# A transformer block in float32 on one core: gate and up projections by one level of Strassen's scheme, on 256 tokens at a time

## The chip, the cores and the metric

The kernel runs on one core of one Trainium2 chip. The metric is the device time of one execution in microseconds (us), lower is better; it is the median of three runs. Shares of a span come from one profiled execution. The core's engines are TensorE (PE, matmuls; its weight loads are shown as PEld), VectorE (DVE), ScalarE (ACT), GpSimd (POOL) and SyncE (SP, which issues most DMAs). They run in parallel, each takes its own instructions in a fixed order, and they wait for each other by semaphores.

## The reference: what is computed

One block of a transformer with 512 tokens and 1024 features: a stick-breaking and a differential attention side by side, gated and projected, then a feed-forward part. The change is in the last two of these lines and in the residual between them:

```python
x = x + einsum('bsd,de->bse', merged, w_out)             # 1024 -> 1024
h2 = _rmsnorm(x, g_ffn)
ff = silu(einsum('bsd,df->bsf', h2, w_ffn_gate)) * einsum('bsd,df->bsf', h2, w_ffn_up)   # 1024 -> 2816
x = x + einsum('bsf,fd->bsd', ff, w_ffn_down)            # 2816 -> 1024
```

Everything is float32.

## The kernel before

Activations are kept with features on the 128 partitions and all 512 tokens along the free axis: x is 8 such blocks, a feed-forward activation 22 (2816 / 128). The 22 are called column tiles below. SBUF is divided by hand: 66 blocks of 128 x 512 in one pool (`B`), 6 buffers of 128 x 1024 for raw weights, and 4 pairs for split weights.

**Float32 as two halves.** PE runs the matmuls on a shorter float format. So each operand is split into h, the rounded value, and l, the rest: `split` (L85) casts on ACT and subtracts on DVE. `mm3` (L202) then makes three matmuls of one product: h by h, h by l, l by h. Activations are split once, weights as they stream in.

**Weights.** `Stream` (L94) holds the list of all weight pieces in order of use, a piece being 128 x 1024, the 8 contraction blocks of one column tile side by side. `next` (L130) splits this piece and the next one and issues the loads of up to 5 further ones on SP's queue.

**The stages that matter here.** In the output projection (L697 to 713), for each of 8 column tiles d, `full_ct(mg)` makes 8 x 3 matmuls of 512 columns into one PSUM bank. DVE adds the old x (loaded again from DRAM) and makes the new residual, which stays in SBUF to the end (`x2`). The norm's gain is multiplied in while the block is split into h2's h and l. ACT squares the block and POOL adds the squares up, for the norm.

In the gate and up stage (L717 to 732), for each of 22 column tiles n, two such products are made, `pg` and `pu`. Behind the first `pg` come the norm's matmul with ones and the factor r2, one per token (L720 to 723). Then DVE multiplies both by r2, ACT applies Silu to one, POOL multiplies the two, and the result is split (L731). In the down stage (L733 to 741), each of 8 output tiles takes 22 x 3 matmuls; DVE adds the residual and the result goes out by DMA.

**Order.** The program gives each instruction its engine. A scheduler orders the instructions of each engine when the program is built, by when it takes their inputs and their buffers to be ready; on the chip this order is fixed. Nothing in these stages is placed by hand.

Of the kernel before, what the change touches and what calls it, by code (L numbers as in the profile page):

```python
# [42 lines left out]
def block_kernel(  # L43
# [40 lines left out]

    def split(h, l, src):  # L85
        a = nc.scalar.copy(out=h, in_=src)  # L86
        b = nc.vector.tensor_tensor(out=l, in0=src, in1=f(h), op=ALU.subtract)  # L87
        return a, b

    def pinned(instrs):  # L90
        for ins in instrs:
            tc.keep_in_program_order(ins)

    class Stream:  # L94
        AHEAD, SPLIT = 5, 2

        def __init__(self, srcs):
            self.srcs, self.raw, self.hl, self.at = srcs, {}, {}, 0
# [8 lines left out]
                    nc.sync.dma_start(out=t[:, :n], in_=src)  # L107

        def split(self, i):
            if i < len(self.srcs) and i not in self.hl:  # L110
                self.load(i)
                t, n = self.raw.pop(i)
                h = wspl.tile([P, 1024], F32R, tag="wh", name=f"wh{i}")
                l = wspl.tile([P, 1024], F32R, tag="wl", name=f"wl{i}")
                split(h[:, :n], l[:, :n], t[:, :n])
                self.hl[i] = (h, l)

        def half(self, kt):
            i, sl = kt // 2, slice((kt % 2) * S, (kt % 2 + 1) * S)
            t, _ = self.raw[i]  # L120
            if kt % 2 == 0:
                h = wspl.tile([P, 1024], F32R, tag="wh", name=f"wh{i}")
                l = wspl.tile([P, 1024], F32R, tag="wl", name=f"wl{i}")
                self.hl[i] = self.part = (h, l)
            h, l = self.part
            pinned(split(h[:, sl], l[:, sl], t[:, sl]))
            if kt % 2:
                self.raw.pop(i)

        def next(self):  # L130
            i = self.at
            self.at += 1
            if i >= KT // 2:
                for j in range(i, i + self.SPLIT):
                    self.split(j)
            for j in range(i, i + self.AHEAD + 1):
                if j not in self.hl:
                    self.load(j)
            return self.hl.pop(i)

    srcs = [w_tc[i, c] for i in range(2) for c in range(4)]
# [22 lines left out]
    for kt in range(KT):  # L164
        t = B(name="xt")
# [521 lines left out]
    for d in range(8):  # L687
        ps = full_ct(o_a)
        nc.vector.tensor_tensor(out=gA[d], in0=gA[d], in1=ps, op=ALU.mult)
        nc.vector.tensor_tensor(out=gA[d], in0=gA[d], in1=mB[d], op=ALU.add)  # L690
        h, l = B(F32R, "mh"), B(F32R, "ml")
        split(h, l, gA[d])
        mg.append((h, l))

    x2, h2 = [], []
    acc = None
    for d in range(8):  # L697
        xr = B(name="xr")
        nc.sync.dma_start(out=xr, in_=xT[:, d])
        ps = full_ct(mg)  # L700
        nc.vector.tensor_tensor(out=xr, in0=ps, in1=xr, op=ALU.add)
        x2.append(xr)
        h, l = B(F32R, "h2h"), B(F32R, "h2l")
        gc = g_ffn[:, d : d + 1]
        nc.scalar.activation(out=h, in_=xr, func=AF.Copy, scale=gc)
        nc.vector.scalar_tensor_tensor(out=l, in0=xr, scalar=gc, in1=f(h), op0=ALU.mult, op1=ALU.subtract)
        h2.append((h, l))
        sq = B(name="x2s")
        nc.scalar.activation(out=sq, in_=xr, func=AF.Square)
        if acc is None:  # L710
            acc = sq
        else:
            nc.gpsimd.tensor_tensor(out=acc, in0=acc, in1=sq, op=ALU.add)

    r2 = B(name="r2")
    ff = []
    for n in range(NF):  # L717
        pg = full_ct(h2)
        if n == 0:
            pn = PS("pn2")  # L720
            nc.tensor.matmul(out=pn, lhsT=ones[:, 0:P], rhs=acc, start=True, stop=True)
            nc.scalar.activation(out=r2, in_=pn, func=AF.Sqrt, scale=1.0 / D, bias=epst)
            nc.vector.reciprocal(out=r2, in_=r2)
        pu = full_ct(h2)
        t1, t2 = B(name="t1"), B(name="t2")
        nc.vector.tensor_tensor(out=t1, in0=pg, in1=r2, op=ALU.mult)
        nc.scalar.activation(out=t1, in_=t1, func=AF.Silu)
        nc.vector.tensor_tensor(out=t2, in0=pu, in1=r2, op=ALU.mult)  # L728
# [75 lines left out]
```

## Time and profile before

| | |
|---|---|
| median of 3 runs (lowest, highest) | 753.12 us (753.03, 753.12) |
| span of the profiled execution, first to last instruction | 751.0 us |
| PE busy, matmuls | 738.1 us (98%), 3406 matmuls |
| PEld busy, weight loads | 611.6 us (81%) |
| DVE busy | 431.8 us (57%) |
| ACT busy | 325.1 us (43%) |
| POOL busy | 103.0 us (14%) |
| DMA | 71.12 MB, 95 GB/s mean |
| granted TensorE clock | 0.998 of 2.4 GHz |

The profiled execution has no time of its own beside its span; the runs' median is 2.1 us above it. An engine's busy time is the union of its instructions' times. Matmuls overlap one another in the records, so PE's pace is read from the starts of its matmuls and not from their durations. In a row of the timeline the first number is the start in us from the start of the span and the second the duration in us; an arrow in square brackets names what ended the engine's idle time before it. L204 is line 204 of the kernel, where a helper's line stands for all its callers; tiles are told by their names, output<-inputs. A row of the windows has the stretch, its length, the busy time (and number of instructions) of PE, PEld, DVE, ACT and POOL in this order, the granted clock as a share of 2.4 GHz, the DMA engines' busy share and GB/s.

### The profile page before, as it was taken

The numbers are of one execution on the slowest core, as the hardware profiler recorded it, in microseconds if no ns is written. First come the engines' busy times: TensorE is split into PE (matmuls) and PEld (weight loads), VectorE is DVE, ScalarE is ACT, GpSimd is POOL, SyncE is SP. The second block draws the span as 40 slices with busy tenths as digits, with TensorE's granted clock in tenths as the row PEclk, the third lists the DMA queues.
The fourth block names the chain that finished last, engine by engine and source line by source line (L and its number), as shares of the span: only waits on it lengthen the run. The fifth ranks groups of instructions, "written<-read, shape, count | busy, mean of one in ns | idle before, by whom it ended". The sixth has DMA issues, their size and how long they took to land.

```text
span 751.0 us, 9018 instructions
## 1 busy us (share of the span) xinstructions
PE 738.1 (98%) x3406; PEld 611.6 (81%) x3406; DVE 431.8 (57%) x648; ACT 325.1 (43%) x514; POOL 103.0 (14%) x139
## 2 busy tenths in 40 slices
PE   8999999999989999999999999999999999999998
PEld 6887887888878878888888888888888888888886
DVE  5856877766687887987446454445545533232220
ACT  6633566877566676544444232323232222222110
POOL 0067000000023223300321011101101111000000
PEclk9999999999999999999999999999999999999999
DMA  8622121211121111244432322332232323333200
GB/s 316 218 98 84 59 83 56 81 61 58 57 84 43 46 39 42 73 152 170 161 120 84 113 84 93 105 103 94 85 112 86 98 83 105 103 118 117 64 14 29
DMA packets 23803, 71.12 MB, mean 95 GB/s; under 512 B 2768, under 2 KB 3408, under 8 KB 23760
## 3 DMA queue, kind: packets, MB, share of 16 engines
q1 hardware_dynamic: 23472, 70.40, 28.0%
q8 instruction: 27, 0.44, 0.2%
q10 hardware_dynamic: 288, 0.15, 0.1%
q14 instruction: 16, 0.13, 0.1%
HBM read 68.44 MB, written 2.10 MB: 94 GB/s over the span
## 4 chain that ended last, share of the span: by engine, by line
PE 89%; DVE 3%; POOL 3%; ACT 2%; issue 2%; DMA 0%; DVEq 0%; POOLq 0%; ACTq 0%
PE pc L204 24%; PE pc L205 24%; PE pc L206 24%; PE pt L221 6%; PE pk L221 3%; PE sc L395 1%; PE sc L394 1%; POOL qn L300 1%; DVE wl L87 1%; PE tb L400 1%; ACT wh L86 1%; PE ta L400 1%; PE av L555 1%; POOL qn L314 1%; PE av L556 1%
## 5 line engine op out<-in xcount | busy, mean ns | idle before, releaser
L86 ACT CAST wh<-raw 128x1024 fp32r<-128x1024 f32 (+2 forms) x136 | 130.9, 963 | 299.1 <-PE pc L205 165.4
L87 DVE TENSOR_TENSOR wl<-raw,wh 128x1024 fp32r<-128x1024 f32 (+2 forms) x136 | 172.7, 1270 | 105.3 <-ACT wh L86 101.2
L204 PE MATMUL pc<-h2h,wh 128*128 128x512 f32 x352 | 137.3, 390 | 0.0
L206 PE MATMUL pc<-h2h,wl 128*128 128x512 f32 x352 | 137.0, 389 | 0.0
L205 PE MATMUL pc<-h2l,wh 128*128 128x512 f32 x352 | 136.9, 389 | 0.0
L204 PE MATMUL pc<-hh,wh 128*128 128x512 f32 x192 | 76.6, 399 | 1.9 <-DVE vs L363 1.5
L205 PEld LDWEIGHTS pc<-h2l,wh 128*128 128x128 f32 x352 | 66.1, 188 | 14.1 <-issue 0.2
L204 PEld LDWEIGHTS pc<-h2h,wh 128*128 128x128 f32 x352 | 66.1, 188 | 14.0 <-issue 0.2
L206 PEld LDWEIGHTS pc<-h2h,wl 128*128 128x128 f32 x352 | 66.1, 188 | 13.5
L206 PE MATMUL pc<-hh,wl 128*128 128x512 f32 x192 | 75.5, 393 | 0.0
L205 PE MATMUL pc<-hl,wh 128*128 128x512 f32 x192 | 75.3, 392 | 0.0
L204 PE MATMUL pc<-fh,wh 128*128 128x512 f32 x176 | 68.5, 389 | 0.0
L205 PE MATMUL pc<-fl,wh 128*128 128x512 f32 x176 | 68.5, 389 | 0.0
L206 PE MATMUL pc<-fh,wl 128*128 128x512 f32 x176 | 68.5, 389 | 0.0
L729 POOL TENSOR_TENSOR t<-t,t 128x512 f32<-128x512 f32 x22 | 30.0, 1363 | 208.5 <-DVE t L728 121.0
L728 DVE TENSOR_TENSOR t<-pc,r 128x512 f32<-128x512 f32 x22 | 15.2, 691 | 67.0 <-PE pc L206 63.2
L204 PEld LDWEIGHTS pc<-hh,wh 128*128 128x128 f32 x192 | 36.4, 190 | 9.2 <-issue 1.7
L206 PEld LDWEIGHTS pc<-hh,wl 128*128 128x128 f32 x192 | 36.2, 189 | 7.8
L205 PEld LDWEIGHTS pc<-hl,wh 128*128 128x128 f32 x192 | 36.4, 190 | 6.7
L530 POOL TENSOR_SCALAR_AFFINE_SELECT om<-om 128x128 f32<-128x128 f32 x32 | 11.4, 356 | 210.4 <-DVE obl L87 138.3
L204 PEld LDWEIGHTS pc<-fh,wh 128*128 128x128 f32 x176 | 33.0, 188 | 6.9
L206 PEld LDWEIGHTS pc<-fh,wl 128*128 128x128 f32 x176 | 33.0, 188 | 6.9
(204 smaller groups left out, 1166.4 us busy)
## 6 DMA issues: line engine op xcount, KB each, us to landing
raw<-w_fg_dram SPq DMA_DIRECT2D x22, 512.0 KB, 3.2
raw<-w_fu_dram SPq DMA_DIRECT2D x22, 512.0 KB, 3.2
raw<-w_gate_dram SPq DMA_DIRECT2D x16, 512.0 KB, 3.2
raw<-w_dn_dram SPq DMA_DIRECT2D x16, 512.0 KB, 3.5
raw<-w_tc_dram SPq DMA_DIRECT2D x12, 512.0 KB, 4.5
raw<-w_ct_dram SPq DMA_DIRECT2D x8, 512.0 KB, 3.3
raw<-w_br_dram SPq DMA_DIRECT2D x16, 256.0 KB, 2.6
raw<-w_out_dram SPq DMA_DIRECT2D x8, 512.0 KB, 3.3
```

What stands on the lines that cost most here:

```text
L86: a = nc.scalar.copy(out=h, in_=src)
L87: b = nc.vector.tensor_tensor(out=l, in0=src, in1=f(h), op=ALU.subtract)
L204: nc.tensor.matmul(out=ps, lhsT=wh, rhs=ah, start=first, stop=False)
L205: nc.tensor.matmul(out=ps, lhsT=wh, rhs=al, start=False, stop=False)
L206: nc.tensor.matmul(out=ps, lhsT=wl, rhs=ah, start=False, stop=last)
L221: nc.tensor.matmul(out=pss[tb], lhsT=hx[:, tb * P : (tb + 1) * P], rhs=wx[:, wsl], start=(kt == 0 and i == 0), stop=(kt == KT - 1 and i == 2),
L300: nc.gpsimd.tensor_tensor(out=q3, in0=q3, in1=gqkt[:, gi : gi + 1, :].broadcast_to([P, 8, 64]), op=ALU.mult,)
L314: nc.gpsimd.tensor_tensor(out=q3[:, :, 0:16], in0=t1, in1=t2, op=ALU.add)
L400: nc.tensor.transpose(out=ps[:, off + (tb - sb) * P : off + (tb - sb + 1) * P], in_=tiles[tb][:, sb * P : (sb + 1) * P], identity=ident,)
L530: nc.gpsimd.affine_select(out=t[:, o + w - P : o + w], in_=t[:, o + w - P : o + w], pattern=[[-1, P]], compare_op=ALU.is_gt, fill=fill, ba ...
L728: nc.vector.tensor_tensor(out=t2, in0=pu, in1=r2, op=ALU.mult)
L729: nc.gpsimd.tensor_tensor(out=t1, in0=t1, in1=t2, op=ALU.mult)
```

## The change: what it does

Two column tiles, gate and up, of the same n form a product of a matrix in 2 x 2 blocks. The activations are cut in two along the contraction (blocks 0 to 3 and 4 to 7) and in two along the tokens (0 to 255, 256 to 511), the weights along the contraction and into up and gate: b11, b21 are up's two halves, b12, b22 gate's. Eight products of 4 blocks and 256 tokens would make it; Winograd's form of Strassen's scheme makes seven, of sums of blocks, and adds up the results.

- **Activations.** Behind the output projection, which takes its column tiles in the order 0, 4, 1, 5, ..., seven operands are built and split: a11, a12, a22 and four sums s1 to s4 (DVE). They hold 28 blocks. The norm's gain is multiplied in on ACT (`y`).
- **Weights.** For each n, `Weights` takes two raw pieces, makes four sums of 512 columns on POOL into two buffers `t13` and `t24` (one of each), and splits up's piece, gate's b22, t13 and t24.
- **Products.** `product` makes 4 x 3 matmuls of 256 columns into half a bank. ACT copies the results of two products to SBUF; DVE, and once POOL, add up the others. Gate's sum comes out negated, which Silu's scale of -1 undoes.
- **Norm.** r2 multiplies gate's sum before Silu; up's r2 is left to the end, where each output of the down stage is multiplied by it (`yo`).
- **ff** is kept whole, and split in a loop behind the 22 tiles. The residual goes to DRAM and is loaded again in the down stage.
- There are 5 raw buffers instead of 6, and 4 pieces are loaded ahead instead of 5.

The core of the diff:

```diff
-N_BLK, N_RAW, N_SPLIT = 66, 6, 4
+N_BLK, N_RAW, N_SPLIT = 66, 5, 4
...
-        AHEAD, SPLIT = 5, 2
+        AHEAD, SPLIT = 4, 2
...
-    x2, h2 = [], []
...
+    half = S // 2
+    lo_t, hi_t = slice(0, half), slice(half, S)
...
+    x2d = nc.dram_tensor("x2_scratch", (KT, P, S), F32, kind="Internal").ap()
...
-    for d in range(8):
+    for d in (0, 4, 1, 5, 2, 6, 3, 7):
         xr = B(name="xr")
         nc.sync.dma_start(out=xr, in_=xT[:, d])
         ps = full_ct(mg)
         nc.vector.tensor_tensor(out=xr, in0=ps, in1=xr, op=ALU.add)
-        x2.append(xr)
-        h, l = B(F32R, "h2h"), B(F32R, "h2l")
-        gc = g_ffn[:, d : d + 1]
-        nc.scalar.activation(out=h, in_=xr, func=AF.Copy, scale=gc)
-        nc.vector.scalar_tensor_tensor(out=l, in0=xr, scalar=gc, in1=f(h), op0=ALU.mult, op1=ALU.subtract)
-        h2.append((h, l))
+        nc.sync.dma_start(out=x2d[d], in_=xr)
+        y = ys[d] = B(name="y")
+        nc.scalar.activation(out=y, in_=xr, func=AF.Copy, scale=g_ffn[:, d : d + 1])
...
+        if d < 4:
+            a11.put(d, y[:, lo_t])
+            continue
+        k = d - 4
+        u, v = ys.pop(k), ys.pop(d)
+        a12.put(k, v[:, lo_t])
+        a22.put(k, v[:, hi_t])
+        sa, sb = B(name="sa"), B(name="sb")
+        nc.vector.tensor_tensor(out=sa[:, lo_t], in0=v[:, hi_t], in1=u[:, hi_t], op=ALU.subtract)
+        nc.vector.tensor_tensor(out=sa[:, hi_t], in0=u[:, lo_t], in1=u[:, hi_t], op=ALU.subtract)
...
+        s1.put(k, sa[:, lo_t])
+        s3.put(k, sa[:, hi_t])
+        s2.put(k, sb[:, lo_t])
+        s4.put(k, sb[:, hi_t])
+
+    class Weights:
+        def __init__(self, n):
+            u, g = ws.take(), ws.take()
+            b11, b21, b12, b22 = u[:, 0:S], u[:, S:1024], g[:, 0:S], g[:, S:1024]
+            t13 = tsum.tile([P, 1024], F32, tag="t13", name=f"t13_{n}")
+            t24 = tsum.tile([P, 1024], F32, tag="t24", name=f"t24_{n}")
+            add = lambda o, a, b: nc.gpsimd.tensor_tensor(out=o, in0=a, in1=b, op=ALU.add)
+            add(t13[:, 0:S], b11, b12)
+            add(t13[:, S:1024], b22, b12)
+            add(t24[:, 0:S], t13[:, 0:S], b22)
+            add(t24[:, S:1024], t24[:, 0:S], b21)
+            uh, ul = self.pair(n, "u")
+            split(uh, ul, u)
+            gh, gl = B(F32R, "gh"), B(F32R, "gl")
+            split(gh, gl, b22)
+            ah, al = self.pair(n, "a")
+            split(ah, al, t13)
+            bh, bl = self.pair(n, "b")
+            split(bh, bl, t24)
...
+    def product(ps, w, a):
+        for kt in range(KT // 2):
+            sl = slice(kt * P, (kt + 1) * P)
+            mm3(ps[:, 0:half], (w[0][:, sl], w[1][:, sl]), a.at(kt), kt == 0, kt == KT // 2 - 1)
...
+    nxt = Weights(0)
     for n in range(NF):
-        pg = full_ct(h2)
+        w = nxt
+        m1 = PS("pc")
+        product(m1, w.b11, a11)
         if n == 0:
             pn = PS("pn2")
...
-        pu = full_ct(h2)
...
+        if n + 1 < NF:
+            nxt = Weights(n + 1)
+        pe, uu, t1, t2 = B(name="pe"), B(name="uu"), B(name="t1"), B(name="t2")
+        nc.scalar.copy(out=pe[:, lo_t], in_=m1[:, 0:half])
+        m5 = PS("m5")
+        product(m5, w.t1, s1)
+        nc.scalar.copy(out=pe[:, hi_t], in_=m5[:, 0:half])
+        m6 = PS("pc")
+        product(m6, w.t2, s2)
+        nc.vector.tensor_tensor(out=uu[:, lo_t], in0=m6[:, 0:half], in1=pe[:, lo_t], op=ALU.add)
+        nc.vector.tensor_tensor(out=t1[:, lo_t], in0=uu[:, lo_t], in1=pe[:, hi_t], op=ALU.add)
+        m7 = PS("m7")
+        product(m7, w.t3, s3)
+        nc.vector.tensor_tensor(out=uu[:, hi_t], in0=m7[:, 0:half], in1=uu[:, lo_t], op=ALU.add)
+        nc.gpsimd.tensor_tensor(out=t1[:, hi_t], in0=uu[:, hi_t], in1=pe[:, hi_t], op=ALU.add)
+        m3 = PS("pc")
+        product(m3, w.b22, s4)
+        nc.vector.tensor_tensor(out=t1[:, lo_t], in0=m3[:, 0:half], in1=t1[:, lo_t], op=ALU.add)
+        nc.vector.tensor_tensor(out=t1, in0=t1, in1=r2, op=ALU.mult)
+        nc.scalar.activation(out=t1, in_=t1, func=AF.Silu, scale=-1.0)
+        m2 = PS("m2")
+        product(m2, w.b21, a12)
+        nc.vector.tensor_tensor(out=t2[:, lo_t], in0=m2[:, 0:half], in1=pe[:, lo_t], op=ALU.add)
+        m4 = PS("pc")
+        product(m4, w.t4, a22)
+        nc.vector.tensor_tensor(out=t2[:, hi_t], in0=m4[:, 0:half], in1=uu[:, hi_t], op=ALU.add)
         nc.gpsimd.tensor_tensor(out=t1, in0=t1, in1=t2, op=ALU.mult)
+        ff.append(t1)
+
+    ws.split(n_down)
+    fs = []
+    for t in ff:
         h, l = B(F32R, "fh"), B(F32R, "fl")
-        split(h, l, t1)
-        ff.append((h, l))
+        split(h, l, t)
+        fs.append((h, l))
     for d in range(8):
+        xr = B(name="xo")
+        nc.sync.dma_start(out=xr, in_=x2d[d])
...
-            nc.vector.tensor_tensor(out=x2[d][:, sl], in0=ps[:, sl], in1=x2[d][:, sl], op=ALU.add)
+            yo = B(name="yo")
+            nc.vector.tensor_tensor(out=yo[:, sl], in0=ps[:, sl], in1=r2[:, sl], op=ALU.mult)
+            nc.vector.tensor_tensor(out=xr[:, sl], in0=yo[:, sl], in1=xr[:, sl], op=ALU.add)
```

## Rows read from the trace of the kernel before

**Rows 1.** Windows by stage: length, then busy time of each engine

```profile
343.70:387.30 43.60, 43.60 (x194) 35.89 (x193) 22.82 (x29) 18.00 (x24) 9.96 (x6) 1.00 0.46 157
387.30:627.50 240.20, 240.20 (x1059) 198.55 (x1058) 120.09 (x111) 74.92 (x92) 30.47 (x22) 1.00 0.29 95
```

**Rows 2.** Timeline of PE in the gate and up stage

```profile
500.40 0.39 PE L204 MATMUL pc<-h2h,wh 128*128 128x512 f32 x1
...
500.63 0.39 PE L205 MATMUL pc<-h2l,wh 128*128 128x512 f32 x1
```

**Rows 3.** Timeline of PE and PEld, 256-column matmuls in the attention part

```profile
229.66 0.28 PE L394 MATMUL sc<-skh,sq 128*128 128x256 f32 x1
229.78 0.28 PE L395 MATMUL sc<-skl,sq 128*128 128x256 f32 x1
...
229.66 0.19 PEld L395 LDWEIGHTS sc<-skl,sq 128*128 128x128 f32 x1
229.78 0.19 PEld L204 LDWEIGHTS pc<-hh,wh 128*128 128x128 f32 x1
```

**Rows 4.** By shape: count, then min/median/max ns, or busy us and mean ns

```profile
L729 POOL TENSOR_TENSOR t<-t,t x22: 1285/1289/2370, 402.2 to 628.6; 128x512 f32<-128x512 f32 x22
...
L314 POOL TENSOR_TENSOR qn<-t,t 128x128 f32<-128x128 f32 x1 | 0.5, 458 | 0.1
...
L87 DVE TENSOR_TENSOR wl<-raw,wh x43: 950/1226/2331, 400.4 to 629.1; 128x1024 fp32r<-128x1024 f32 x42, 128x768 fp32r<-128x768 f32 x1
...
L87 DVE TENSOR_TENSOR fl<-t,fh x21: 676/678/693, 404.1 to 626.2; 128x512 fp32r<-128x512 f32 x21
...
L87 DVE TENSOR_TENSOR tc<-tc,tc 128x256 fp32r<-128x256 f32 x12 | 5.0, 416 | 1.0 <-ACT tc L86 1.0
...
L86 ACT CAST wh<-raw x44: 840/1053/1056, 387.3 to 622.1; 128x1024 fp32r<-128x1024 f32 x43, 128x768 fp32r<-128x768 f32 x1
...
L86 ACT CAST tc<-tc 128x256 fp32r<-128x256 f32 x12 | 4.5, 376 | 4.5 <-PE tc L400 4.5
```

**Rows 5.** Timeline of DVE, then POOL, from 410 us

```profile
410.16 0.69 DVE L728 TENSOR_TENSOR t<-pc,r 128x512 f32<-128x512 f32 x1 [3.31 <-PE pc L206]
411.06 2.30 DVE L87 TENSOR_TENSOR wl<-raw,wh 128x1024 fp32r<-128x1024 f32 x1 [0.21 <-ACT wh L86]
...
411.00 1.29 POOL L729 TENSOR_TENSOR t<-t,t 128x512 f32<-128x512 f32 x1 [7.54 <-DVE t L728]
```

**Rows 6.** Timeline of POOL, then DVE, from 606 us

```profile
606.86 2.37 POOL L729 TENSOR_TENSOR t<-t,t 128x512 f32<-128x512 f32 x1 [9.59 <-ACT wh L86]
...
606.86 1.23 DVE L87 TENSOR_TENSOR wl<-raw,wh 128x1024 fp32r<-128x1024 f32 x1 [0.17 <-ACT wh L86]
```

**Rows 7.** Timeline of DVE, then POOL, from 58.5 us

```profile
58.87 0.68 DVE L296 TENSOR_TENSOR qn<-pk,st 128x512 f32<-128x512 f32 x1
...
58.66 1.28 POOL L300 TENSOR_TENSOR qn<-qn,gqkt 128x512 f32<-128x512 f32 x1
```

**Rows 8.** Timeline of DVE, then ACT, behind the output projection

```profile
387.49 0.69 DVE L701 TENSOR_TENSOR xr<-pc,xr 128x512 f32<-128x512 f32 x1 [2.65 <-PE pc L206]
...
395.83 3.35 DVE L723 RECIPROCAL r<-r 128x512 f32<-128x512 f32 x1 [0.78 <-ACT r L722]
...
388.26 0.72 ACT L705 ACTIVATE h2h<-xr,colt 128x512 fp32r<-128x512 f32 x1
388.89 0.62 ACT L709 ACTIVATE x2s<-xr 128x512 f32<-128x512 f32 x1
```

**Rows 9.** DMA issues: count, KB each, median us to landing

```profile
raw<-w_fg_dram SPq DMA_DIRECT2D x22, 512.0 KB, 3.2
```

**Rows 10.** Windows around two idle times of PE, columns as in rows 1

```profile
217.00:219.20 2.20, 0.00 (x0) 0.00 (x0) 1.88 (x5) 1.08 (x3) 0.82 (x2) 1.00 0.35 136
219.20:222.50 3.30, 3.28 (x12) 2.90 (x13) 2.55 (x4) 2.55 (x5) 0.11 (x1) 0.56 0.28 94
...
269.00:271.80 2.80, 2.01 (x12) 1.62 (x10) 2.42 (x6) 2.75 (x7) 0.42 (x2) 1.00 0.38 94
```

More of the change, by code (lines that the diff above doesn't have):

```diff
@@ L65, in block_kernel @@
     blk = ctx.enter_context(tc.tile_pool(name="blk", bufs=N_BLK))
+    tsum = ctx.enter_context(tc.tile_pool(name="tsum", bufs=1))
     small = ctx.enter_context(tc.tile_pool(name="small", bufs=4))
@@ L109, in split @@
         def split(self, i):
-            if i < len(self.srcs) and i not in self.hl:
+            if i < len(self.srcs) and i not in self.hl and not n_plain <= i < n_down:
                 self.load(i)
@@ L128, in half, with take @@
                 self.raw.pop(i)
+        def take(self):
+            i = self.at
+            self.at += 1
+            for j in range(i, i + self.AHEAD):
+                if j not in self.hl:
+                    self.load(j)
+            return self.raw.pop(i)[0]
         def next(self):
@@ L153, in block_kernel @@
     srcs += [w_br[d, 0] for d in range(8)]
-    srcs += [w_out[d] for d in range(8)]
+    srcs += [w_out[d] for d in (0, 4, 1, 5, 2, 6, 3, 7)]
+    n_plain = len(srcs)
     for n in range(NF):
-        srcs += [w_fg[n], w_fu[n]]
+        srcs += [w_fu[n], w_fg[n]]
+    n_down = len(srcs)
     for d in range(8):
@@ L693, in block_kernel, with __init__, at, put @@
         mg.append((h, l))
-    x2, h2 = [], []
+    half = S // 2
+    lo_t, hi_t = slice(0, half), slice(half, S)
+    class Operand:
+        def __init__(self, name):
+            self.h = [B(F32R, name + "h") for _ in range(2)]
+            self.l = [B(F32R, name + "l") for _ in range(2)]
+        def at(self, kt):
+            sl = slice((kt % 2) * half, (kt % 2 + 1) * half)
+            return self.h[kt // 2][:, sl], self.l[kt // 2][:, sl]
+        def put(self, kt, src):
+            split(*self.at(kt), src)
+    a11, a12, a22 = Operand("a11"), Operand("a12"), Operand("a22")
+    s1, s2, s3, s4 = Operand("s1"), Operand("s2"), Operand("s3"), Operand("s4")
+    x2d = nc.dram_tensor("x2_scratch", (KT, P, S), F32, kind="Internal").ap()
+    ys = {}
     acc = None
-    for d in range(8):
+    for d in (0, 4, 1, 5, 2, 6, 3, 7):
         xr = B(name="xr")
@@ new lines, in block_kernel, with pair @@
+        nc.vector.scalar_tensor_tensor(
+            out=sb[:, lo_t], in0=sa[:, lo_t], scalar=-1.0, in1=u[:, lo_t], op0=ALU.mult, op1=ALU.subtract
+        )
+        nc.vector.scalar_tensor_tensor(
+            out=sb[:, hi_t], in0=v[:, lo_t], scalar=-1.0, in1=sb[:, lo_t], op0=ALU.mult, op1=ALU.subtract
+        )
+        s1.put(k, sa[:, lo_t])
[21 more added lines that the diff above has]
+            split(bh, bl, t24)
+            lo, hi = slice(0, S), slice(S, 1024)
+            self.b11, self.b21 = (uh[:, lo], ul[:, lo]), (uh[:, hi], ul[:, hi])
+            self.b22 = (gh, gl)
+            self.t1, self.t3 = (ah[:, lo], al[:, lo]), (ah[:, hi], al[:, hi])
+            self.t2, self.t4 = (bh[:, lo], bl[:, lo]), (bh[:, hi], bl[:, hi])
+        def pair(self, n, c):
+            return (
+                wspl.tile([P, 1024], F32R, tag="wh", name=f"wh{c}{n}"),
+                wspl.tile([P, 1024], F32R, tag="wl", name=f"wl{c}{n}"),
+            )
@@ L723, in block_kernel @@
             nc.vector.reciprocal(out=r2, in_=r2)
-        pu = full_ct(h2)
[L725 to L728, printed above, removed]
+        if n + 1 < NF:
+            nxt = Weights(n + 1)
+        pe, uu, t1, t2 = B(name="pe"), B(name="uu"), B(name="t1"), B(name="t2")
+        nc.scalar.copy(out=pe[:, lo_t], in_=m1[:, 0:half])
@@ L729, in block_kernel @@
+        m4 = PS("pc")
+        product(m4, w.t4, a22)
+        nc.vector.tensor_tensor(out=t2[:, hi_t], in0=m4[:, 0:half], in1=uu[:, hi_t], op=ALU.add)
         nc.gpsimd.tensor_tensor(out=t1, in0=t1, in1=t2, op=ALU.mult)
+        ff.append(t1)
+    ws.split(n_down)
+    fs = []
+    for t in ff:
         h, l = B(F32R, "fh"), B(F32R, "fl")
-        split(h, l, t1)
-        ff.append((h, l))
+        split(h, l, t)
+        fs.append((h, l))
     for d in range(8):
-        ps = full_ct(ff[0:8], last=False)
@@ L735, in block_kernel @@
-        full_ct(ff[8:16], ps=ps, first=False, last=False)
-        full_ct(ff[16:22], ps=ps, first=False, last=True)
+        xr = B(name="xo")
+        nc.sync.dma_start(out=xr, in_=x2d[d])
+        ps = full_ct(fs[0:8], last=False)
+        full_ct(fs[8:16], ps=ps, first=False, last=False)
+        full_ct(fs[16:22], ps=ps, first=False, last=True)
         parts = 2 if d == 7 else 1
@@ L739, in block_kernel @@
             sl = slice(i * S // parts, (i + 1) * S // parts)
-            nc.vector.tensor_tensor(out=x2[d][:, sl], in0=ps[:, sl], in1=x2[d][:, sl], op=ALU.add)
-            (nc.sync, nc.scalar)[i].dma_start(out=out[d * P : (d + 1) * P, sl], in_=x2[d][:, sl])
+            yo = B(name="yo")
+            nc.vector.tensor_tensor(out=yo[:, sl], in0=ps[:, sl], in1=r2[:, sl], op=ALU.mult)
+            nc.vector.tensor_tensor(out=xr[:, sl], in0=yo[:, sl], in1=xr[:, sl], op=ALU.add)
+            (nc.sync, nc.scalar)[i].dma_start(out=out[d * P : (d + 1) * P, sl], in_=xr[:, sl])
 def kernel(**inputs):
```

## The prediction

> **What bounds the kernel now.** I read the windows by stage first. In the gate and up stage, from 387.3 to 627.5 us, PE is busy for all 240.20 us, at full granted clock; DVE is busy for 120.09 us and POOL for 30.47 [rows 1]. So PE sets the pace there and the other engines have time to spare. Then the pace of PE itself: in its timeline one 512-column matmul starts at 500.40 and the next at 500.63; over the window's 1056 of them (and one more for the norm) it is 0.227 us each [rows 1, 2]. One column tile takes 2 x 8 x 3 = 48 of them, 10.9 us, and 22 tiles take 239.7 us, which is the window. Last I looked for places where DVE and POOL are at work at once (rows 5 to 7), since the change gives both of them more.
>
> **PE's side of the change.** Seven products of 4 x 3 matmuls with 256 columns are 84 matmuls per tile, each with a weight load of its own. The kernel before has such matmuls in its attention part: they start 0.120 us apart, and their loads also 0.120 [rows 3]. So 84 x 0.120 = 10.08 us per tile; 22 tiles, and about 1 us for the norm's own matmul, make 222.8 us. That is 17.4 less than 240.2 and all there is to gain; a 256-column matmul costs not half of 0.227 but 0.0065 more.
>
> **What it adds for DVE and POOL, per tile.** POOL gets four weight sums and the product t1*t2, each 512 wide, 1.29 us, and one sum 256 wide. Between 0.46 us for 128 columns and 1.29 for 512 [rows 4] that one is about 0.73 (an estimate on the line between these two). Sum 5 x 1.29 + 0.73 = 7.18 us.
> DVE gets three subtractions 1024 wide (1.22 us), one 512 wide (0.68), the product with r2 (0.68) and the sum of uu and pe (256 wide, 0.42), all with both inputs in SBUF [rows 4]: 3 x 1.22 + 2 x 0.68 + 0.42 = 5.44 us. It has five sums more with one input in PSUM, 256 wide at 0.42: 2.1 us. ACT has three casts at 1.05, one and the Silu at about 0.62, two short copies at 0.38: 5.2 us.
> Each of them alone fits into 10.08 us. The question is whether DVE and POOL fit together.
>
> **They don't run side by side.** Where POOL's product of two SBUF tiles started at 411.00, DVE's subtraction of two SBUF tiles, started at 411.06, took 2.30 us and not 1.22 [rows 5]: its own 1.22 us began only at 412.14, 0.15 before POOL's end. Where both started at 606.86, it was POOL that took 2.37 and not 1.29 [rows 6]: it began 1.08 us late, 0.14 before DVE's end. So one waits for nearly the whole of the other. DVE's product of a PSUM tile at 58.87 lay inside a POOL instruction that ran from 58.66 to 59.94; they took 0.68 and 1.28, and neither lost anything [rows 7]. So it is DVE's instructions with two SBUF inputs that exclude POOL's: they share one way into SBUF, "the port" below.
> What an instruction keeps of the port is then its duration less 0.15 us. DVE: 3 x 1.07 + 2 x 0.53 + 0.27 = 4.54. POOL: 5 x 1.14 + 0.58 = 6.28. Together 10.82 us per tile, more than PE's 10.08. In whole durations it is 5.44 + 7.18 = 12.62. The pace lies between these two ends, if both queues always have something ready at the low one.
> I take 11.5, a little above the middle of the lower half. Laid out in order, a tile has about four places where the port stands empty for a hand-over: t1*t2 waits for the last sum from PSUM, POOL's short sum for DVE's, the product with r2 for POOL's, and the next weight sums, which have one buffer, for the last subtraction. Each costs some 0.1 to 0.2 us (rows 5: DVE's sum ends at 410.85 and POOL, which waits for it, starts at 411.00), so 10.82 + 0.7.
> The weights of the first tile can be made while the output projection still runs (43.6 us, DVE 22.82 and POOL 9.96 busy [rows 1]): 3 x 1.07 + 0.53 + 4 x 1.14 = 8.3 us. So the loop takes 22 x 11.5 - 8.3 = 244.7 us against 240.2: +4.5.
>
> The Trainium skill, page "SBUF — State Buffer", section "Who interferes with whom", has the same two engines share a port pair, as a lock kept for the full instruction. The rows let go 0.15 us earlier. By the page the sum would be 12.62 per tile, which is the second rival below. It also says that a DVE instruction with one SBUF input doesn't contend, and rows 7 agree.
>
> **Start of the loop.** Before, the last block of the residual was needed only by the last of 8 steps of the first product; now the chain behind the last output matmul is xr (0.69), y (0.72), a difference (0.42) and its split (0.38 + 0.42) [rows 4, 8], with hand-overs about 3.1 us, while the first product takes 12 x 0.120 = 1.44 us and three quarters of the second another 1.1. If PE keeps the norm's matmul behind the first product, it waits for xr, y, the square (0.62) and POOL's sum (1.29 or more): 3.7 us, so 2.3 of idle. Then come the Sqrt and DVE's reciprocal of 3.35 us [rows 8], which lay under a product of 5.4 us (24 x 0.227); now it holds DVE's port work back by 1 to 2 us. Together 1 to 6 us, and I take 3.5.
>
> **Start of the down stage.** The 22 splits of ff are moved out of the loop: 0.62 on ACT and 0.68 on DVE each, as long as PE needs for one step of three matmuls (3 x 0.227 = 0.68). The last tile makes no next weights, which leaves about 8 us of the port free, and some blocks are free by then: 66 less 28 of the operands, 22 of ff and some 7 others is 9, so four pairs. If nothing were made early, the first step waits 1.3 us, and three weight splits of 1.22 come on top of 15 us: 3 us in all. Bounds 0 and 3; I take 1.
>
> **The rest.** In the output projection two blocks now give DVE two residual sums, two weight splits and eleven short ones, 2 x 0.69 + 2 x 1.22 + 11 x 0.42 = 8.4 us, and ACT 2 x (0.72 + 0.62) + 7 x 0.38 + 2 x 1.05 = 7.4, of PE's 10.9; of the port that is 2.1 + 3.0 for DVE and 2.3 for POOL's two sums, 7.4. So it stays at PE's pace. SP's queue gets eight stores and eight loads of 256 KB. A store waits for its residual sum, and the weight loads queued behind it wait too; they land in 3.2 us [rows 9] and are issued four tiles, over 20 us, ahead, also with a raw buffer less: nothing, up to 1 us where the first load of the residual is late. In the tail each half has two sums for one: 2 x 0.42, less what they overlap: +0.7.
>
> **Sum.** 751.0 + 4.5 + 3.5 + 1 + 0.7 = 760.7 us of span. The runs' median is 753.12, 2.1 us over the profiled span, which lie ahead of the first and behind the last instruction; nothing of the change is there. 762.8, so 763 us.
>
> **Rivals.**
> *PE keeps the pace* (not slower). The port's waits fall into time in which neither engine is needed: weights are made a tile ahead, so a late one costs nothing until PE asks for it. For it: each engine alone has 3 us per tile to spare. Against it: a stock of one tile is used up after some ten tiles at 0.74 a tile. The loop then takes 222.8: 751.0 - 17.4 + 5.2 + 2.1 = 741. It decides for faster from a pace of 11.06 downward, where 22 p - 8.3 + 5.2 equals 240.2; the low end of the port's sum, 10.82, would still do it, at 748.
> *The queues add up.* Each engine takes its instructions in a fixed order. DVE's product with r2 stands behind POOL's short sum, and that may stand behind weight sums; whenever one of them waits so for the other, the 0.15 us of each instruction in which it doesn't use the port lie bare, and the pace is that of the whole durations, 12.62: 22 x 12.62 - 9.5 = 268.1, +27.9, so 786 us; more still, if PE's banks wait for it too. For it: six changes of hand per tile. Against it: rows 5 and 6 hand over without loss.
> *The clock falls.* Where PE stood idle for 2.2 us at 217, its granted clock was 0.56 for the 3.3 us behind (1.2 GHz for most of it); between 269 and 271.8, with 0.8 us idle, it stayed at 1.00 [rows 10]. At a pace of 11.5 PE stands idle 1.4 us per tile, between these. Half clock for 3.4 us of each tile costs up to 1.7 us; part of it lies in the idle time, about 1 us stays: +22, so 785 us.
>
> **Chances.** Port-bound at 10.8 to 12: 0.55, with 748 to 774 (0.10 of it faster, 0.06 the same). PE keeps the pace: 0.16. Queues: 0.21. Clock: 0.08. A change of 0.2%, 1.5 us, is about what a measurement of this kernel can tell from none. Faster 0.26, same 0.06, slower 0.68. The likeliest case alone is 750 to 774; the range takes in half of the first rival and most of the others: 744 to 793.
>
> **What would show it.** In the profile after: a matmul with 256 columns starts 0.120 us behind the last; PE idle over 1 us per tile in the loop, ended by a subtraction of DVE's on a split weight; DVE's 1024-wide subtractions and POOL's sums with means well over 1.23 and 1.29; a loop of 240 to 250 us; PE idle for 2 to 4 us behind the output projection. I am wrong if PE has no idle time in the loop (it is then faster), if the idle time is ended by something else than a weight split (PSUM, a DMA), or if most of the loss lies outside the loop.

## The result, and the profile after

The changed kernel takes 787.3 us (median of 4 runs, 787.29 to 787.5), the kernel before 753.1 beside it (4 runs, 751.27 to 753.12): a ratio of 1.0462, 95% interval 1.0447 to 1.0477. The profiled execution has a span of 785.6 us; PE is busy for 730.0 us of it, DVE for 594.8 (before 431.8), POOL for 281.2 (before 103.0). Slower by 34 us, where 10 had been forecast.

The windows of the changed kernel by stage, columns as in [rows 1]: output projection, gate and up, down stage with the tail:

```profile
342.80:386.40 43.60, 43.60 (x194) 35.90 (x193) 31.11 (x44) 22.06 (x39) 13.71 (x10) 1.00 0.46 157
386.40:658.90 272.50, 231.63 (x1852) 224.94 (x1850) 257.08 (x267) 114.12 (x175) 204.54 (x128) 0.97 0.26 90
658.90:785.60 126.70, 120.73 (x528) 98.84 (x528) 48.92 (x62) 31.41 (x42) 1.61 (x1) 1.00 0.32 99
```

The gate and up stage took 240.2 us before [rows 1] and takes 272.5: nearly the whole loss. The first products of its 22 column tiles start at 386.36, 412.92, 423.97, 434.05, 448.41, and from 460.16 to 648.17 every 11.75 us; the down stage starts at 658.87. So the first tile takes 26.6 us, the next three 35.5 together, and the rest 11.75 each, with 10.7 for the last.

The costliest groups that answer to [rows 4] and [rows 5] (count, busy time and mean ns, then the idle time before them and what ended it):

```profile
L217 PE MATMUL pc<-s2h,wlb 128*128 128x256 f32 x88 | 26.9, 305 | 27.0 <-DVE wlb L88 27.0
L839 POOL TENSOR_TENSOR t<-t,t 128x512 f32<-128x512 f32 x22 | 48.5, 2207 | 6.6 <-DVE t L838 3.9
L88 DVE TENSOR_TENSOR wlu<-raw,whu 128x1024 fp32r<-128x1024 f32 x22 | 47.6, 2165 | 0.1
L88 DVE TENSOR_TENSOR wlb<-t,whb 128x1024 fp32r<-128x1024 f32 x22 | 42.7, 1941 | 1.5 <-ACT whb L87 1.4
```

One subtraction, wlb, ends 27.0 us of PE's idle time. Two of DVE's three wide (1024-column) subtractions, wlu and wlb, take 1.9 to 2.2 us instead of 1.23, and POOL's product 2.2 instead of 1.29; the third, wla, keeps its 1.21. In a tile of the steady stretch PE waits once, for wlb:

```profile
557.17 0.28 PE L216 MATMUL pc<-s2l,whb 128*128 128x256 f32 x1
558.87 0.39 PE L217 MATMUL pc<-s2h,wlb 128*128 128x256 f32 x1 [1.42 <-DVE wlb L88]
```

The same tile on DVE:

```profile
552.98 1.21 DVE L88 TENSOR_TENSOR wla<-t,wha 128x1024 fp32r<-128x1024 f32 x1
554.11 0.41 DVE L830 TENSOR_TENSOR t<-pc,t 128x256 f32<-128x256 f32 x1
554.82 1.76 DVE L831 TENSOR_TENSOR t<-t,r 128x512 f32<-128x512 f32 x1 [0.30 <-POOL t L827]
556.50 0.41 DVE L835 TENSOR_TENSOR t<-m,pe 128x256 f32<-128x256 f32 x1
556.83 1.98 DVE L88 TENSOR_TENSOR wlb<-t,whb 128x1024 fp32r<-128x1024 f32 x1
558.74 0.41 DVE L838 TENSOR_TENSOR t<-pc,uu 128x256 f32<-128x256 f32 x1
559.07 2.26 DVE L88 TENSOR_TENSOR wlu<-raw,whu 128x1024 fp32r<-128x1024 f32 x1
561.25 1.78 DVE L88 TENSOR_TENSOR gl<-raw,gh 128x512 fp32r<-128x512 f32 x1
562.96 0.41 DVE L822 TENSOR_TENSOR uu<-pc,pe 128x256 f32<-128x256 f32 x1
563.47 0.99 DVE L823 TENSOR_TENSOR t<-uu,pe 128x256 f32<-128x256 f32 x1
564.39 0.41 DVE L826 TENSOR_TENSOR uu<-m,uu 128x256 f32<-128x256 f32 x1
564.73 1.21 DVE L88 TENSOR_TENSOR wla<-t,wha 128x1024 fp32r<-128x1024 f32 x1
```

and on POOL:

```profile
553.20 1.59 POOL L827 TENSOR_TENSOR t<-uu,pe 128x256 f32<-128x256 f32 x1 [0.76 <-DVE uu L826]
554.75 1.28 POOL L771 TENSOR_TENSOR t<-raw,raw 128x512 f32<-128x512 f32 x1
555.99 1.74 POOL L771 TENSOR_TENSOR t<-raw 128x512 f32<-128x512 f32 x1
558.96 1.29 POOL L771 TENSOR_TENSOR t<-t,raw 128x512 f32<-128x512 f32 x1 [1.23 <-DVE wlb L88]
560.21 2.28 POOL L839 TENSOR_TENSOR t<-t,t 128x512 f32<-128x512 f32 x1
562.45 1.74 POOL L771 TENSOR_TENSOR t<-t,raw 128x512 f32<-128x512 f32 x1
```

Read side by side: at 559.07 wlu starts 0.11 us behind POOL's sum, and takes 2.26 us; gl at 561.25 meets the product t1*t2 and takes 1.78 where 0.68 is its own. DVE's sums with an input in PSUM (L830, L835, L838, L822, L826) keep their 0.41 beside any of POOL's. And DVE is never idle for longer than 0.30 us in this tile.

The start of the stage. The sums that make the last three blocks of the residual (`xr`), and some of what stands between them (timeline of DVE):

```profile
384.13 0.69 DVE L732 TENSOR_TENSOR xr<-pc,xr 128x512 f32<-128x512 f32 x1 [0.86 <-DMA xr<-xT_dram]
384.74 2.01 DVE L88 TENSOR_TENSOR wlb<-t,whb 128x1024 fp32r<-128x1024 f32 x1
...
388.45 1.48 DVE L750 TENSOR_TENSOR sa<-y,y 128x256 f32<-128x256 f32 x1
...
393.08 1.23 DVE L88 TENSOR_TENSOR wlu<-raw,whu 128x1024 fp32r<-128x1024 f32 x1
...
394.56 0.68 DVE L732 TENSOR_TENSOR xr<-pc,xr 128x512 f32<-128x512 f32 x1
...
399.17 0.69 DVE L732 TENSOR_TENSOR xr<-pc,xr 128x512 f32<-128x512 f32 x1 [0.97 <-DMA xr<-xT_dram]
```

SP's queue beside it:

```profile
385.23 0.42 SPq L730 DMA_DIRECT2D xr<-xT_dram  x1
394.37 0.33 SPq L108 DMA_DIRECT2D raw<-w_fu_dram  x1
395.27 0.33 SPq L733 DMA_DIRECT2D x_scratch<-xr  x1
395.65 0.42 SPq L730 DMA_DIRECT2D xr<-xT_dram  x1
```

and the windows of the first tile:

```profile
386.40:396.90 10.50, 3.12 (x20) 2.43 (x18) 8.82 (x14) 4.24 (x9) 4.40 (x4) 0.79 0.23 70
396.90:412.90 16.00, 11.46 (x68) 9.74 (x68) 12.49 (x17) 8.57 (x16) 4.11 (x4) 0.71 0.35 119
```

PE's last output matmul starts at 386.13, but block 7 of the old residual is loaded only at 395.65, behind the store of block 3, and its sum comes at 399.17; before, the last sum was at 387.49, on the heels of PE [rows 8]. Block 3's sum, at 394.56, doesn't wait for its load, which was issued at 385.23 (the loads there land in about 3.4 us). It stands in DVE's queue behind block 6's chain and two weight subtractions of the first tile, and from 384.13 to 394.56 DVE is never idle for more than 0.1 us. Of the first tile's 26.5 us PE is busy for 14.6, and at a granted clock of 0.71 to 0.79.

### The profile page after: what moved, and what is told of

It reads as the page before. It is cut to its first block, busy times and chain, and to the rows that moved or that the text cites. A ratio compares the mean times of both kernels' runs of the same rounds, so it can differ in the third digit from the quotient of the medians.

```text
span 785.6 us, 11191 instructions
## 1 busy us (share of the span) xinstructions
PE 730.0 (93%) x4198; PEld 637.1 (81%) x4198; DVE 594.8 (76%) x847; ACT 378.0 (48%) x630; POOL 281.2 (36%) x249
## 5 line engine op out<-in xcount | busy, mean ns | idle before, releaser
L88 DVE TENSOR_TENSOR wl<-raw,wh 128x1024 fp32r<-128x1024 f32 (+2 forms) x92 | 99.6, 1084 | 75.9 <-ACT wh L87 68.0
L87 ACT CAST wh<-raw 128x1024 fp32r<-128x1024 f32 (+2 forms) x92 | 84.6, 920 | 145.4 <-PE pc L216 90.6
L541 POOL TENSOR_SCALAR_AFFINE_SELECT om<-om 128x128 f32<-128x128 f32 x32 | 11.4, 356 | 208.8 <-ACT om L538 200.2
L771 POOL TENSOR_TENSOR t<-t,raw 128x512 f32<-128x512 f32 x44 | 66.3, 1507 | 24.8 <-DVE wlb L88 24.5
L217 PE MATMUL pc<-s2h,wlb 128*128 128x256 f32 x88 | 26.9, 305 | 27.0 <-DVE wlb L88 27.0
L839 POOL TENSOR_TENSOR t<-t,t 128x512 f32<-128x512 f32 x22 | 48.5, 2207 | 6.6 <-DVE t L838 3.9
L771 POOL TENSOR_TENSOR t<-raw,raw 128x512 f32<-128x512 f32 x22 | 28.9, 1315 | 53.8 <-DMA raw<-w_fg_dram 37.6
L87 ACT CAST wha<-t 128x1024 fp32r<-128x1024 f32 x22 | 23.1, 1052 | 51.7 <-PE m L216 39.8
L88 DVE TENSOR_TENSOR wlu<-raw,whu 128x1024 fp32r<-128x1024 f32 x22 | 47.6, 2165 | 0.1
L88 DVE TENSOR_TENSOR wlb<-t,whb 128x1024 fp32r<-128x1024 f32 x22 | 42.7, 1941 | 1.5 <-ACT whb L87 1.4
L831 DVE TENSOR_TENSOR t<-t,r 128x512 f32<-128x512 f32 x22 | 35.6, 1619 | 6.9 <-POOL t L827 6.8
```

The costliest lines, as they stand in the source:

```text
L541: nc.gpsimd.affine_select(out=t[:, o + w - P : o + w], in_=t[:, o + w - P : o + w], pattern=[[-1, P]], compare_op=ALU.is_gt, fill=fill, ba ...
L771: add = lambda o, a, b: nc.gpsimd.tensor_tensor(out=o, in0=a, in1=b, op=ALU.add)
L831: nc.vector.tensor_tensor(out=t1, in0=t1, in1=r2, op=ALU.mult)
```

## The experiments

Ratios are to the kernel before, run beside each. "Pace" is the time from one column tile's first product to the next one's in the steady stretch.

**1. POOL's sums made harmless.** `add` writes a constant three times instead of adding, so the four weight sums are left out.

```diff
-            add = lambda o, a, b: nc.gpsimd.tensor_tensor(out=o, in0=a, in1=b, op=ALU.add)
+            add = lambda o, a, b: [nc.gpsimd.memset(o, 1.0) for _ in range(3)]
```

> The four weight sums on POOL are left out; in their place POOL writes constants into the same two buffers, three writes of 128x512 for each sum, which read nothing from SBUF. DVE and ACT do what they did. Theory (DVE and POOL exclude each other at the port): without the sums the port is wanted 10.82 - 4 x 1.14 = 6.3 us per tile, less than PE's 84 x 0.120 = 10.08, so the loop's pace falls from 11.75 to 10.1 to 10.4 us per tile and DVE's 1024-wide subtractions come back from 1.9 to 2.2 us to about 1.3; the whole 785.6 us of span less 22 x 1.5 = 33, so about 750 to 757. Rival (POOL's own load, or the fixed order of the queues, sets the pace): POOL stays as busy as before, so the pace stays at 11.3 to 11.75 and the span over 775.

Measured: 750.2 us (one run), pace 10.08 from the third tile on. In its windows POOL is as busy as in the changed kernel (83.3 there), and PE is never idle:

```profile
500.00:600.00 100.00, 100.00 (x835) 100.00 (x835) 83.04 (x110) 46.65 (x71) 83.48 (x139) 1.00 0.31 105
```

So it is what POOL's sums read or how, and not that POOL is at work, which costs the 1.67 us per tile. The constants also need no weights, so by itself this run doesn't part the port from the sums' own waits; experiment 2 keeps the sums with their inputs and moves them off POOL, and its pace is the same. The first tile still takes 23.3 us.

**2. All of the loop's POOL work on DVE.** The four sums, the sum of uu and pe and t1*t2.

```diff
-            add = lambda o, a, b: nc.gpsimd.tensor_tensor(out=o, in0=a, in1=b, op=ALU.add)
+            add = lambda o, a, b: nc.vector.tensor_tensor(out=o, in0=a, in1=b, op=ALU.add)
...
-        nc.gpsimd.tensor_tensor(out=t1[:, hi_t], in0=uu[:, hi_t], in1=pe[:, hi_t], op=ALU.add)
+        nc.vector.tensor_tensor(out=t1[:, hi_t], in0=uu[:, hi_t], in1=pe[:, hi_t], op=ALU.add)
...
-        nc.gpsimd.tensor_tensor(out=t1, in0=t1, in1=t2, op=ALU.mult)
+        nc.vector.tensor_tensor(out=t1, in0=t1, in1=t2, op=ALU.mult)
```

> All of POOL's work in the loop goes to DVE: four weight sums, the short sum and the product t1*t2. Theory (exclusion): a DVE instruction costs the port less than POOL's of the same size and meets nobody there; back to back DVE then needs about 6.65 + 4 x 0.60 + 0.34 + 0.60 = 10.0 us per tile, beside PE's 10.08. Pace 10.2 to 10.8 instead of 11.75, no DVE subtraction over 1.25 us, whole time 787.3 less 22 x 1.2 = 26, so about 761 (755 to 768). Rival (DVE's amount of work is the limit and POOL relieves it): DVE gets 3.3 us more per tile, pace over 12.5, time over 800.

Measured: 754.9 us, ratio 1.0046 (1.003 to 1.0061), pace 10.08: the theory's way, and further than its 755 to 768 and 10.2 to 10.8. DVE's timeline gives what each of its instructions takes of its queue when nothing disturbs it, read from start to start:

```profile
523.69 1.23 DVE L88 TENSOR_TENSOR wlb<-t,whb 128x1024 fp32r<-128x1024 f32 x1
524.83 0.42 DVE L822 TENSOR_TENSOR uu<-pc,pe 128x256 f32<-128x256 f32 x1
525.16 0.68 DVE L771 TENSOR_TENSOR t<-raw,raw 128x512 f32<-128x512 f32 x1
525.76 0.42 DVE L823 TENSOR_TENSOR t<-uu,pe 128x256 f32<-128x256 f32 x1
```

1.14 us for 1024 columns, 0.60 for 512, 0.33 for 256. Six more instructions per tile for DVE took 32 us off the time. The first tile takes 26.5 us still: a second, separate loss.

**3 and 4. The old residual's loads on ACT's queue**, in the changed kernel and in the one of experiment 2.

```diff
-        nc.sync.dma_start(out=xr, in_=xT[:, d])
+        nc.scalar.dma_start(out=xr, in_=xT[:, d])
```

> The loads of the old residual in the output projection go out on ACT's queue instead of SP's, nothing else. Theory (the loop's start is late because these loads stand on SP behind weight loads that wait for raw buffers): the last residual sum comes at 388 to 391 us instead of 399.2, the first tile takes 14 to 17 us instead of 26.6, the time falls by 9 to 12, so 775 to 778. Rival (the start is late because DVE and POOL block each other there, or blocks run out): the residual sums stay 8 to 12 us behind PE, and the time within 3 us of 787.3.

> Both: POOL's loop work on DVE, residual loads on ACT's queue. If both theories hold the gains add up: 787.3 - 26 - 10 = about 751 (743 to 760), which would be level with the kernel before. If the late start was DVE's and POOL's blocking, the second part adds nothing to the first: 761.

Measured: 789.2 us, ratio 1.049 (1.0474 to 1.0507), and 756.7, ratio 1.0051 (1.0036 to 1.0066). No gain; the theory that SP's queue holds the loads up falls. In the first of them the last two loads are issued at 394.77 and 399.22 on ACT: on either queue they stand behind the chain of the block before.

**5 and 6. All eight loads ahead of the output projection's loop**, alone and with the edit of experiment 2.

```diff
+    xrs = {}
     for d in (0, 4, 1, 5, 2, 6, 3, 7):
-        xr = B(name="xr")
-        nc.sync.dma_start(out=xr, in_=xT[:, d])
+        xrs[d] = B(name="xr")
+        nc.sync.dma_start(out=xrs[d], in_=xT[:, d])
+    for d in (0, 4, 1, 5, 2, 6, 3, 7):
+        xr = xrs[d]
         ps = full_ct(mg)
```

> The changed kernel with the loads of all eight blocks of the old residual issued ahead of the output projection's loop; POOL keeps its sums. My theory: the late start of the gate and up loop (26.6 us in its first tile, against a pace of 11.75) comes from the last two blocks of the old residual, whose load is issued only behind the chain of the block before and lands at 399, 12 us behind the last output matmul. Then the last two residual sums on DVE come at 385 to 389 instead of 394.6 and 399.2, the first tile takes 15 to 18 us, the pace stays 11.75, and the time is 775 to 780 us. The rival, that DVE's and POOL's work on the first tiles' weights sets the start: the sums come earlier, and the first tile still takes 24 us or more, so 784 to 788 us.

> The same, with all of POOL's sums and products of the loop on DVE as well, so that nothing meets at the port. The two losses are separate by my theory: the pace is 10.08 (32 us gained, as measured) and the first tile gives another 8 to 11: 743 to 747 us, faster than the kernel before at 752.6. By the rival (DVE's own queue of weight work sets the start, and it is longer here) the first tile stays at 24 us or more: 752 to 755 us.

Measured: 781.05 us, ratio 1.0385 (1.0366 to 1.0405), and 744.5, ratio 0.9893 (0.9872 to 0.9913). The first tile takes 18.8 and 15.1 us. The last two sums come at 387.67 and 391.25 in the first version, and in the second so:

```profile
385.15 0.68 DVE L735 TENSOR_TENSOR xr<-pc,xr 128x512 f32<-128x512 f32 x1
...
389.09 0.68 DVE L735 TENSOR_TENSOR xr<-pc,xr 128x512 f32<-128x512 f32 x1
```

The loads were worth 6 us alone and 10 with a free POOL, and the second version is 1.1% faster than the kernel before: the seven products do pay. In the first, which I had at 775 to 780, 7 us over the pace stay in the first tile: PE waits 3.2 us there for POOL's sum of squares and 1.7 for a11. The edit does more than move the loads: the scheduler also orders DVE anew, and block 3's sum, which didn't wait for its load, comes 6.9 us earlier, now ahead of wlb and wlu. How much of the gain is the loads and how much that order, no run separates.

**7. The norm's matmul later in the first tile** (ahead of the third product), in the version of experiment 6: the five lines from `if n == 0` move down.

> The same, with the norm's own matmul, Sqrt and reciprocal moved in the first tile from behind the first product to ahead of the third product, so that PE does not stand at the norm's matmul while it could run the second product. My theory: the norm's matmul stops PE until the last square and POOL's sum of squares are done, some 2 us behind the last block; 1 to 3 us less than the run without this move, so 741 to 745 us. If the first tile is held by the splits of the last blocks alone, no difference (within 1 us); if the reciprocal comes too late for the scaling with r2, 1 to 3 us more.

Measured: 743.8 us, ratio 0.9884 (0.9861 to 0.9906): no difference that could be told. PE no longer waits there for the sum of squares, but 1.9 us for s1, which hangs on the same last blocks; so where the norm's matmul stands doesn't set what is left of the loss.

**8 and 9. Part of POOL's work on DVE**, with the early loads: the sum of uu and pe and the product t1*t2 (L827 and L839), then the four weight sums instead, each as in experiment 2.

> The early loads of the old residual; POOL keeps the four weight sums of each tile, and its sum of uu and pe and its product t1*t2 go to DVE. A tile's holds of the port in the changed kernel add up to 10.82 us, with 0.93 idle. Two POOL instructions leave (1.14 + 0.58) and two of DVE's come (0.53 + 0.27): 9.90, and between 0 and 0.93 idle. If the holds of both engines simply add up, the pace is 10.08 (PE's own) to 10.83: 744 to 761 us, against 781 with both on POOL. The rival, that POOL's weight sums alone do the damage, whatever the sum is (each of DVE's three wide subtractions meets one): the pace stays above 11.3, so over 771 us.

> The other half: POOL keeps the sum of uu and pe and the product t1*t2, and the four weight sums go to DVE. Holds: 10.82 less 4 x 1.14 plus 4 x 0.53 = 8.4 us, well under 10.08 even with 0.93 idle. The pace is PE's 10.08, and the time that of the run with everything on DVE, 743 to 748 us. The rival, that a product of POOL's in the chain of the banks (t1*t2 waiting, with DVE behind it) holds the pace: 11 or more, so over 764 us.

Measured: 778.1 us, ratio 1.033 (1.0308 to 1.0353), and 751.8, ratio 0.999 (0.9973 to 1.0007). Paces 11.77 and 10.52: both above my ends, and the first not under the pace with everything on POOL. That is the pace of 8's rival; for its reason see experiment 10, where POOL's weight sums are the same. The window of 8 shows more; the third busy time is DVE's:

```profile
500.00:600.00 100.00, 87.14 (x709) 85.31 (x709) 98.62 (x109) 41.16 (x62) 55.97 (x35) 1.00 0.26 85
```

The port had 1.9 us per tile to spare by my sum (9.90 of 11.77), and DVE had almost nothing: it is busy for 98.6%. So the pace is not the port's but DVE's, which executes in order and can't go on to a sum from PSUM while an instruction ahead of it stands for POOL.

**10. Two of DVE's sums that don't use the port, given to ACT**, in the version of experiment 8.

```diff
-        nc.vector.tensor_tensor(out=uu[:, lo_t], in0=m6[:, 0:half], in1=pe[:, lo_t], op=ALU.add)
+        nc.scalar.copy(out=uu[:, lo_t], in_=m6[:, 0:half])
...
-        nc.vector.tensor_tensor(out=uu[:, hi_t], in0=m7[:, 0:half], in1=uu[:, lo_t], op=ALU.add)
+        nc.scalar.copy(out=uu[:, hi_t], in_=m7[:, 0:half])
```

> POOL keeps the four weight sums, DVE has the products, the old residual is loaded early (778 us without the edit, pace 11.77), and two of DVE's sums with an input in PSUM (the two parts of uu) become copies on ACT, which leaves out one addend each. They use no port, and POOL's work is unchanged. My theory now: the pace is the length of DVE's own queue, its own work of 7.5 us per tile plus 4.1 in which it stands for POOL's sums; it was idle for 0.17. So 0.65 to 0.85 less per tile, a pace of 10.9 to 11.1, and 760 to 765 us. The rival, that the port and its hand-overs set the pace, has the same work at the port as before: 11.7, and 776 to 779 us.

Measured: 757.0 us, ratio 1.0049 (1.0032 to 1.0065), pace 10.57. With POOL's work and my sum for the port as before, 0.67 us less in DVE's queue took 1.2 off the pace, more than I had expected. DVE is now busy without a gap:

```profile
500.00:600.00 100.00, 97.86 (x799) 96.03 (x798) 100.00 (x106) 52.34 (x86) 57.47 (x38) 1.00 0.29 101
```

**11. Two buffers for each weight sum**, in the version of experiment 5.

```diff
-N_BLK, N_RAW, N_SPLIT = 66, 5, 4
+N_BLK, N_RAW, N_SPLIT = 63, 5, 4
...
-    tsum = ctx.enter_context(tc.tile_pool(name="tsum", bufs=1))
+    tsum = ctx.enter_context(tc.tile_pool(name="tsum", bufs=2))
```

> The changed kernel with the early loads of the old residual (781 us, pace 11.75) and two buffers for each of the weight sums in place of one (three blocks fewer, 63 for 66), so that POOL's sums wait no more for DVE's subtraction of the tile before. All the work at the port is the same. My theory: POOL's sums can then run while DVE does its narrow sums from PSUM, some 1.6 us per tile, and DVE stands less: a pace of 10.4 to 11.4, and 754 to 774 us. The rival, that POOL's sums meet DVE's subtractions all the same, since DVE is at work nearly all the time: 11.6 or more, 777 to 784 us.

Measured: 785.2 us, ratio 1.0424 (1.0405 to 1.0443), pace still 11.76. My theory missed; the rival's pace held. DVE is busy for 96.3 of 100 us, and its instructions meet POOL's as before. The time lies even over the rival's, since the first tile takes 23.8 us and not 18.8; why, stays open.

## Why the prediction was wrong

**Right.** A matmul every 0.120 us and 10.08 us per tile, as in [rows 3] (experiments 1, 2 and 6 run at it). DVE's instructions with two inputs in SBUF exclude POOL's, as in [rows 5] and [rows 6]; PE's idle time of about 1.4 us per tile is ended by a split weight; the kernel is slower. The first rival, PE keeps the pace, fell. So did the third: with that idle time the granted clock is 1.00 in the steady tiles, and in this stage it fell only in the first one. Of my signs two failed: the loop takes 272.5 us and not 240 to 250, and PE's idle time behind the output projection is 11.9 us and not 2 to 4.

**The terms.** From the first product to the down stage the sum had 248.2 us (244.7 + 3.5) and the trace has 272.5:

| term | forecast | measured | difference |
|---|---|---|---|
| pace, 22 tiles | 11.5 | 11.75 | +5.5 |
| first weights made ahead | -8.3 | -1.05 (last tile 10.70), +0.25 (tiles 2 to 21) | +7.5 |
| start of the loop | +3.5 | +14.8 (26.56 less 11.75) | +11.3 |
| down stage and tail | +1.7 | +3.3 | +1.6 |

With 0.9 us less ahead of the loop that is 25.0, and 785.6 - 760.7 is 24.9.

**The start is the step that failed most.** I followed the chain behind the last output matmul, with every instruction at its own duration and its inputs there, and put the loads of the old residual at "nothing, up to 1 us". But DVE takes its instructions in order: the chain of each block had become long, the first tiles' weights stood between its links, POOL's sums stretched both (1.48 us for differences of 0.41), and each load is placed behind the chain of the block before. In time from the start of one matmul to the next, over the usual 0.12, the first tile's 16.5 us too many are 5.1 for s2, 4.8 for a11, 4.0 for the sum of squares and 1.9 for the norm's own matmul; of these waits only that for the sum of squares needs block 7, whose load is late; s2 and a11 wait for DVE's queue. Experiment 5 gives 7.8 us of the first tile back, and experiments 3 and 4 show that it isn't SP's queue. In experiment 2 the first tile is as long, with the sums in DVE's own queue, and with the weight sums left out (experiment 1) it is 3.2 us shorter, so POOL's stretching is the smaller part. No run puts the first tile's weights behind the whole chain. In experiment 6, 5.0 us over 10.08 are left, and PE's starts account for 4.8: 1.6 for a11, 1.9 for the sum of squares, 0.8 for the norm's matmul, 0.4 for s2.

```profile
389.23 0.39 PE L216 MATMUL pc<-a11l,whu 128*128 128x256 f32 x1 [1.34 <-DVE a11l L88]
...
392.58 1.13 PE L813 MATMUL pn<-x2s,ones 128*128 128x512 f32 x2 [1.78 <-POOL x2s L744]
```

**The credit for weights made ahead wasn't there.** Tiles 2 and 3 took 11.05 and 10.08, 2.4 us less than the pace, and tile 4 14.36, 2.6 more. What stays is 1.05 us in the last tile, which makes no next weights. I read it so: in the steady stretch DVE's queue is full, whatever lies in stock; no run tests this by itself.

**The pace came out near by luck.** I made the port the bound: 10.82 us of holds and some hand-overs. Experiments 8 and 10 have the same port sum, 9.90, and paces of 11.77 and 10.57. What orders them is DVE's queue, its own work by experiment 2's rows (3 x 1.14 + 2 x 0.60 + 6 x 0.33 = 6.6 in the changed kernel) plus the time it stands for POOL:

| per tile, us | port by my sum | DVE's own | POOL's holds | pace | pace less own, of the holds |
|---|---|---|---|---|---|
| changed kernel | 10.82 | 6.6 | 6.28 | 11.75 | 82% |
| 8, weight sums on POOL | 9.90 | 7.5 | 4.56 | 11.77 | 94% |
| 10, as 8, with two of DVE's sums less | 9.90 | 6.9 | 4.56 | 10.57 | 80% |
| 9, short sum and product on POOL | 8.4 | 9.0 | 1.72 | 10.52 | 88% |
| 2, none | 7.5 | 9.9 | 0 | 10.08 (PE) | - |

DVE pays for 80 to 94% of POOL's holds: it is busy for 96.7 to 100 of 100 us in the first four, and all of its work in a tile but three to five sums from PSUM is instructions with two SBUF inputs. What sets the share within these bounds stays open. The sums from PSUM (5 x 0.33 us per tile) belong to this queue too; I had left them out because they use no port. The second rival said that each engine takes its instructions in order and waits for the other, which is this mechanism; but it priced the pace at 12.62, and its 786 us is near the result only because the losses at the start make up for that. The Trainium skill, page "SBUF — State Buffer", section "SBUF: two separate sides", has the port kept for a whole instruction. Kept for whole recorded durations it would be taken for 12.62 us per tile; the trace's 11.75 is less, so that reading isn't borne out.

**Where the gain went.** The 17 us that the matmuls save, as worked out (240.2 to 222.8), were given back at the pace (1.67 x 21 = 35 us) and at the start (16.5 over PE's 10.08). The two are nearly separate: experiment 2 gives 32 us back and experiment 5 alone 6, experiment 6, with both, 43.

## What to carry to other kernels

When two engines exclude each other at a port, don't add up the port: add, for the in-order engine that has the fuller queue, its whole work, also what doesn't use the port, and most of the other engine's holds (80 to 94% in these kernels). Work moved to an idle engine that shares the port can so cost the busy one more than doing it itself (a 512-column sum: 0.60 us on DVE, against most of 1.14 of standing). And where a stage's last block becomes the next stage's first need, follow its chain through the queues with the loads, not by the durations of its links; a load that depends on nothing is issued ahead of the loop.

## What the hardware showed unexpectedly

Which of POOL's instructions get in DVE's way can be seen within experiment 1, between 500 and 600 us:

```profile
L88 DVE TENSOR_TENSOR gl<-raw,gh 128x512 fp32r<-128x512 f32 x10 | 17.9, 1786 | 0.0
L88 DVE TENSOR_TENSOR wlb<-t,whb 128x1024 fp32r<-128x1024 f32 x10 | 12.3, 1226 | 0.5
L88 DVE TENSOR_TENSOR wlu<-raw,whu 128x1024 fp32r<-128x1024 f32 x10 | 12.2, 1220 | 0.0
```

POOL's constant writes of 512 columns (0.48 us of its time each, POOL busy for 83 of 100 us) left wlb and wlu at 1.23 and 1.22 us, where its sums of the same size made them 1.9 to 2.3; gl, which still meets POOL's product, takes 1.79 instead of 0.68. PE's idle time of 1.4 us in each tile left the granted clock at 1.00 in the steady stretch (11.4 us idle between 500 and 600 us). In the first tile, with 11.9 us idle, it was 0.79 and 0.71 in the mean, and there are stretches at the lower level (1.2 GHz) in which 256-column matmuls start 0.21 us apart instead of 0.12.
